# Residual rows of two matrix products added by accumulating DMA transfers instead of by VectorE

## The chip, the cores and the metric

The kernel runs on one core of one Trainium2 chip. A core has a matrix engine (TensorE, "PE" in the profile), three engines for elementwise work (VectorE "DVE", ScalarE "ACT", GpSimd "POOL"), and SyncE ("SP"), which in this kernel issues DMA transfers. Matmuls read SBUF and accumulate in PSUM banks. The engines run side by side and wait for each other through semaphores, and each works through its own queue in order. The metric is the time of one execution on the device in microseconds; lower is better.

## The reference

One decoder layer on 512 tokens of width 2048, in float32. What matters here:

```
h   = rms_norm(x, norm1_g)
mix = concat(gla_mixer(...), dilated_mixer(...))      # from h @ w_in
x   = x + mix @ w_out                                 # output product + residual
h2  = rms_norm(x, norm2_g)
x   = x + (silu(h2 @ w_gate) * (h2 @ w_up)) @ w_down  # last product + residual
```

w_out is 2048 x 2048, w_gate and w_up are 2048 x 5632, w_down is 5632 x 2048. Both additions of x are residuals: the product's result and the rows of x so far are added elementwise.

## The kernel before, in words

**Products by Strassen's scheme.** Every large product is cut into blocks of 512 output columns by 256 tokens and computed by the seven-product scheme of Strassen and Winograd. A `Pair` is one such unit: two blocks of 512 columns for two halves of 256 tokens, from the products P1, P5, P6, P3, P7, P2, P4 in this order (`PRODUCTS`). Each product runs over `op.groups` groups of rows (4, and 3 in the last two pairs of the last product). One product and one group is an item.

**An item.** The weights are loaded in quarters of 512 KB (`load_quarter`, line 222; tiles `wa` to `wd`), some are subtracted from each other on VectorE (line 256), ScalarE rounds the result to the matrix engine's format (`wh`, line 331), VectorE computes the rest (`wl`, line 335), and TensorE does 12 matmuls (line 361): 8 with `wh`, 4 with `wl`. `wh` and `wl` have two buffers each. The left operand is split into tiles `AA` and `AS` the same way (lines 174 and 175).

**Seeds and closes.** P1, P5 and P6 are first products: when one ends, `seeds` has ScalarE copy its two PSUM banks into SBUF tiles `seed` (line 280, or line 282 with a scale), m = 0 one item and m = 1 two items later. P2, P7 and P3 end a block: `close` adds the bank to the seed on VectorE (line 294, or 298 with a scale), and then `final(half, which, tiles, None)` gets the finished tiles. P1's seed is closed after P2, P5's after P7, and P6's after P3, the product that follows it. P4 ends the fourth block without a seed; there `final` gets the bank itself.

**Residuals.** In the output product (`final_out`, two pairs) and the last product (`final_down`, six pairs: three slices of the inner dimension by two column halves), `final` adds residual rows: rows of x in the first; rows of the stored x (`x1_d`) or of the sums so far (`y_d`) in the second. `begin` calls `ahead` three items after the start of P3, P7, P2 and P4, which loads two tiles of 128 x 512 from DRAM into the single buffers `q` and `k` (`residual_loads`, line 1313). `residual` then adds them on VectorE: to the closed seed (line 1325) for three blocks of a pair, and the bank to the loaded tile (line 1322) for P4's. The results are stored (lines 1354, 1541 and 1539).

**What the output product does besides.** Its `final` also squares the tiles for the next norm (ScalarE, line 1356), scales them with `prox` (line 1333; `prox` is computed on GpSimd, lines 158 and 159, from the first pair's sums), turns them on TensorE (line 1120) and sends them to DRAM tensors `xn_d`, from where they come back as operand parts of the gate and up products (`r`, `top`, `T`, `v`, lines 1184 and 1228). The first gate and up pair needs all of them. In the last product, operand parts come from `p_d` and `S_d` the same way while the pair before still runs.

**What sets the order.** After the first pair a scheduler places each engine's instructions, in the order of the calls as far as inputs and buffers allow by its own estimate. Each engine, and SyncE's queue of DMA issues, then runs in that order; an issue that waits for a buffer holds those behind it.

Of the kernel before, what the change touches and what calls it, by code (L numbers as in the profile page):

```python
# [14 lines left out]
ALU = mybir.AluOpType  # L15
# [3 lines left out]
P = 128  # L19
# [16 lines left out]
CLOSES = {"P3": (0, 1), "P7": (1, 1), "P2": (0, 0), "P4": (1, 0)}  # L36
# [71 lines left out]
def block_kernel(ctx: ExitStack, tc: tile.TileContext, ins, out):  # L108
    nc = tc.nc
    x, w_in, w_out, w_gate, w_up, w_down = (  # L110
        ins[n] for n in ("x", "w_in", "w_out", "w_gate", "w_up", "w_down")
    )
# [15 lines left out]
    def nm(s):  # L128
        uid[0] += 1
        return f"{s}_{uid[0]}"  # L130
# [7 lines left out]
    def work(tag, shape=(P, 512), bufs=1):  # L138
        return mp.tile(list(shape), F32, name=nm(tag), tag=tag, bufs=bufs)
# [6 lines left out]
    load = nc.sync.dma_start  # L146
# [10 lines left out]
    def rsqrt_mean(dst, src, n):  # L157
        nc.gpsimd.tensor_scalar(dst, src, 1.0 / n, EPS, op0=ALU.mult, op1=ALU.add)
        nc.gpsimd.tensor_tensor(dst, dst, mhalf[:, : dst.shape[-1]], op=ALU.pow)
# [69 lines left out]
    def unfolded(t):  # L229

        return t.rearrange("p (a b) -> p b a", b=2)

    def halves(t):
        return t.rearrange("p (b a) -> p b a", b=2)

    class Pair:
# [25 lines left out]
        def begin(self, prod):  # L262
            if prod == "P1":
                X = self.accs()
                self.dst = {"P1": X, "P6": X, "P7": X, "P4": X}
            elif prod == "P5":
                self.dst["P5"] = self.dst["P3"] = self.accs()
            elif prod == "P2":
                self.dst["P2"] = self.accs()
            ahead = getattr(self.final, "ahead", None)  # L270
            if ahead and prod in CLOSES:
                later(3, lambda: ahead(*CLOSES[prod]))

        def seeds(self, src, half):
            res = []

            def one(m):
                t = cpool.tile([P, 512], F32, name=nm("seed"), tag="C")
                if self.scale is None:
                    nc.scalar.copy(halves(t), unfolded(src[m]))  # L280
                else:
                    nc.scalar.activation(  # L282
                        halves(t), unfolded(src[m]), AF.Copy, scale=self.scale(half, m)
                    )
                res.append(t)

            later(1, lambda: one(0))
            later(2, lambda: one(1))
            return res
# [18 lines left out]
        def end(self, prod):  # L308
            src = self.dst[prod]
            if prod in ("P1", "P5", "P6"):  # L310
                self.held[prod] = self.seeds(src, int(prod == "P5"))
            elif prod == "P4":
                later(1, lambda: self.final(1, 0, None, src), hold=True)
            else:
                which = {"P3": "P6", "P7": "P5", "P2": "P1"}[prod]
                self.close(self.held[which], src, *CLOSES[prod])
# [181 lines left out]
    def later(units, fn, hold=False):  # L498

        deferred.append([units, fn, hold])  # L500
# [182 lines left out]
    for g in range(4):  # L683
        for b in (2 * g, 2 * g + 1):
            if g < 3:
                t = apool.tile([P, 2, 512], F32, name=nm("xT"), tag="A")
# [487 lines left out]

        soon(rest, 2)

    final_gate.ahead = onorm_load

    def part(src, half):
        def get(t=None):  # L1180
# [8 lines left out]
    def early_jobs(op, groups, tops, flip):  # L1189

        h0, h1 = (1, 0) if flip else (0, 1)
        jobs = [op.early(g, part(tops[g], h0), part(tops[g], h1)) for g in groups]
        next(jobs[0])
        yield
        for i, job in enumerate(jobs):
            if i + 1 < len(jobs):
                next(jobs[i + 1])
            next(job)
            yield 0.5
            next(job)  # L1200
            yield 0.5
# [103 lines left out]
    prox = const([P, 4], "prox")  # L1305
    rs2 = const([P, 4], "rs2")

    def residual_loads(rows, c0, src):

        res = []  # L1310
        for m in range(2):
            r = work(("q", "k")[m])
            load(r, src(rows[m], c0))
            res.append(r)
        return res

    def residual(tiles, acc_, rest):
        res = []
        for m in range(2):
            r = rest[m]  # L1320
            if tiles is None:
                nc.vector.tensor_tensor(halves(r), unfolded(acc_[m]), halves(r), op=ALU.add)
                res.append(r)
            else:
                nc.vector.tensor_tensor(tiles[m], tiles[m], r, op=ALU.add)  # L1325
                res.append(tiles[m])
        return res

    def scaled_store(tiles, rows, half, dsts, k0, tags=None):
        xs = []  # L1330
        for m in range(2):
            s = work(tags[m]) if tags else work("L", bufs=2)
            nc.scalar.activation(s, tiles[m], AF.Copy, scale=prox[:, rows[m] : rows[m] + 1])
            xs.append(s)
        return lambda: transposed_store(xs, half, dsts, g2[:, k0 : k0 + 4])

    def final_out(second):
        rest_of = {}

        def ahead(half, which):  # L1340
            tok = 1 - half
            rest_of[half, which] = residual_loads(
                [2 * tok, 2 * tok + 1], 512 * (2 * second + which),
                lambda t, c: x[t * P : (t + 1) * P, c : c + 512],
            )

        def final(half, which, tiles, acc_):
            tok = 1 - half
            rows = [2 * tok, 2 * tok + 1]
            ch = 2 * second + which  # L1350
            tiles = residual(tiles, acc_, rest_of.pop((half, which)))
            for m in range(2):
                t = rows[m]
                store(x1_d[t][:, 512 * ch : 512 * ch + 512], tiles[m])
                jk = work("st", (P, DV), bufs=2).bitcast(mybir.dt.bfloat16)
                nc.scalar.activation(
                    jk, tiles[m], AF.Square, accum_out=ss2[:, t, ch : ch + 1]
                )
            if second:
                turn = scaled_store(tiles, rows, tok, xn_d[2 * ch : 2 * ch + 2], 4 * ch)  # L1360

                def rest():
                    turn()
                    if which == 1 and half == 1:
                        background.append(early_jobs(opn, (2, 3), tops, False))
                        background.append(late_jobs(opn, ((2, 3),), tops, bots, False))

                later(2, rest)
                if which == 0 and half == 1:
                    output_scales()  # L1370
            elif which == 0 and half == 1:
                nc.vector.tensor_tensor(part2, ss2[:, :, 0], ss2[:, :, 1], op=ALU.add)
                rsqrt_mean(prox, part2, D // 2)
                background.append(first_columns())
                background.append(operand_jobs(opn, tops, bots, 0, 2))

        final.ahead = ahead
        return final

    def first_columns():  # L1380
        places = [(ch, tok) for ch in range(2) for tok in range(2)]
# [30 lines left out]
    def output_scales():  # L1412
        tmp2 = const([P, 4], "tmp2")
        nc.vector.tensor_tensor(tmp2, ss2[:, :, 2], ss2[:, :, 3], op=ALU.add)
        nc.vector.tensor_tensor(tmp2, tmp2, part2, op=ALU.add)
        rsqrt_mean(rs2, tmp2, D)
        nc.gpsimd.tensor_scalar(part2, part2, 2.0 / D, EPS, op0=ALU.mult, op1=ALU.add)
        nc.gpsimd.tensor_tensor(part2, part2, phalf, op=ALU.pow)
        nc.gpsimd.tensor_tensor(rs2, rs2, part2, op=ALU.mult)
# [92 lines left out]
    for j in range(11):  # L1512
        c = slice(512 * j, 512 * j + 512)
# [6 lines left out]
    y_d = [dram([P, D], f"y_d{t}") for t in range(4)]  # L1520

    def final_down(i, np_):
        rest_of = {}
        prev = x1_d if i == 0 else y_d

        def ahead(half, which):
            rest_of[half, which] = residual_loads(
                [2 * half, 2 * half + 1], 512 * (2 * np_ + which),
                lambda t, c: prev[t][:, c : c + 512],
            )  # L1530

        def final(half, which, tiles, acc_):
            rows = [2 * half, 2 * half + 1]
            c0 = 512 * (2 * np_ + which)
            tiles = residual(tiles, acc_, rest_of.pop((half, which)))
            for m in range(2):
                t = rows[m]
                if i == 2:
                    store(out[t * P : (t + 1) * P, c0 : c0 + 512], tiles[m])
                else:  # L1540
                    store(y_d[t][:, c0 : c0 + 512], tiles[m])

        final.ahead = ahead
        return final

    for i in range(3):
        g0 = 4 * i
        rows_d = [(512 * (g0 + g), 512 * (g0 + g) + 256) for g in range(opd[i].groups)]
        for np_ in range(2):
            c = 1024 * np_  # L1550
# [51 lines left out]
```

## Time and profile before

| | |
|---|---|
| median of 3 runs | 1977.21 us |
| lowest, highest | 1974.11, 1977.57 us |
| profiled execution | 1975.93 us, of it the span 1974.1 us |
| granted TensorE clock in it | 0.996 |
| TensorE, VectorE, ScalarE, GpSimd busy | 1932.0, 1655.0, 1094.1, 58.7 us |
| DMA moved | 360.45 MB, 57.3% of the DMA engines' time on SyncE's queue |

Times of rows are microseconds from the span's start. Of the two stages that the change touches, the output product lies at about 570 to 720, and the last product at about 1570 to 1970. A group's row gives the line, the engine, the operation, the tile written and those read, the shape, the count, then busy time and mean nanoseconds of one, then the idle time of the engine ahead of these instructions and what ended it. A row of the waits view gives who waited for whom: total, times, longest. A row of the timeline gives start, duration, engine, line, and in a bracket the idle time just before.

### The profile page before, as it was taken

Reading aid. Unit: us, or ns where it says so; the run is one execution under the profiler, and the core shown is the slowest. Engines: PE = TensorE matmul, PEld = TensorE weight load, DVE = VectorE, ACT = ScalarE, POOL = GpSimd, SP = SyncE. Lnnn points to the kernel's source line nnn. Section 1 sums busy time; section 2 is a strip of 40 time slices with the busy share of each in tenths; the row PEclk is TensorE's granted clock in tenths of the full one; section 3 lists DMA queues with packets and bytes.
Section 4 is the critical chain, followed back from the end, with each engine's and each line's share of the span. In section 5 each row is a group of like instructions: output and inputs, shape, how many; then the busy total and the mean of one; then the engine's idle time right before and its main releaser. Section 6 shows DMA issues by size and latency. Waiting matters only on the chain.

```text
span 1974.1 us, 25791 instructions
## 1 busy us (share of the span) xinstructions
PE 1932.0 (98%) x9226; PEld 1671.6 (85%) x9226; DVE 1655.0 (84%) x1850; ACT 1094.1 (55%) x1600; POOL 58.7 (3%) x81
## 2 busy tenths in 40 slices
PE   7999999999999999999999999999999999999998
PEld 6888888888878877888888888888888888888887
DVE  7997887868789789878878878878879989989987
ACT  6664564566766666545545545445446646546443
POOL 0000230010000000000000000000000000000000
PEclk9999999999999999999999999999999999999999
DMA  8358365374666685554554554554555855855762
GB/s 277 113 170 276 106 186 157 127 213 133 214 205 203 215 278 163 179 166 129 182 166 132 176 165 129 175 163 132 172 163 168 294 204 180 301 179 178 248 213 75
DMA packets 237113, 360.45 MB, mean 183 GB/s; under 512 B 18246, under 2 KB 96783, under 8 KB 236984
## 3 DMA queue, kind: packets, MB, share of 16 engines
q1 hardware_dynamic: 236776, 358.72, 57.3%
q8 instruction: 72, 1.18, 0.3%
q14 instruction: 57, 0.47, 0.1%
q10 hardware_dynamic: 208, 0.08, 0.0%
HBM read 296.59 MB, written 64.51 MB: 183 GB/s over the span
## 4 chain that ended last, share of the span: by engine, by line
PE 79%; DVE 8%; DMA 7%; issue 3%; ACT 2%; SPq 1%; POOL 1%; DVEq 0%; ACTq 0%
PE acc L361 71%; DVE wl L335 3%; PE acc L429 3%; DVE wa L256 1%; PE bank L1120 1%; PE bank L978 1%; ACT wh L331 1%; DMA wc<-in_w_in 1%; DVE AS L175 1%; DMA T<-p_d 1%; DMA x<-in_x 1%; DMA q<-y_d 0%; PE bank L1010 0%; DMA xn_d<-oT 0%; DVE seed L1325 0%
## 5 line engine op out<-in xcount | busy, mean ns | idle before, releaser
L361 PE MATMUL acc<-wh,AS 128*128 128x512 f32 x3008 | 712.0, 379 | 0.0
L361 PEld LDWEIGHTS acc<-wh,AS 128*128 128x128 f32 x3008 | 569.1, 189 | 81.7 <-ACT wh L331 0.6
L331 ACT CAST wh<-wa 128x1024 fp32r<-128x1024 f32 x376 | 393.6, 1048 | 384.2 <-PE acc L361 359.5
L361 PE MATMUL acc<-wh,AA 128*128 128x512 f32 x2256 | 536.4, 381 | 5.6 <-ACT wh L331 5.4
L335 DVE TENSOR_TENSOR wl<-wa,wh 128x1024 fp32r<-128x1024 f32 x376 | 457.4, 1220 | 72.0 <-ACT wh L331 46.5
L361 PEld LDWEIGHTS acc<-wh,AA 128*128 128x128 f32 x2256 | 426.7, 190 | 70.0 <-ACT wh L331 9.1
L361 PE MATMUL acc<-wl,AS 128*128 128x512 f32 x1504 | 395.7, 386 | 7.9 <-DVE wl L335 7.2
L361 PEld LDWEIGHTS acc<-wl,AS 128*128 128x128 f32 x1504 | 278.9, 189 | 61.7 <-DVE wl L335 20.9
L361 PE MATMUL acc<-wl,AA 128*128 128x512 f32 x1128 | 299.0, 388 | 6.1 <-DVE wl L335 6.1
L361 PEld LDWEIGHTS acc<-wl,AA 128*128 128x128 f32 x1128 | 210.7, 190 | 38.7 <-DVE wl L335 9.0
L331 ACT CAST wh<-wb 128x1024 fp32r<-128x1024 f32 x94 | 98.6, 1049 | 127.4 <-PE acc L361 122.7
L331 ACT CAST wh<-wc 128x1024 fp32r<-128x1024 f32 x94 | 98.4, 1047 | 106.8 <-PE acc L361 102.2
L331 ACT CAST wh<-wd 128x1024 fp32r<-128x1024 f32 x94 | 98.4, 1048 | 105.8 <-PE acc L361 102.3
L256 DVE TENSOR_TENSOR wa<-wc,wa 128x1024 f32<-128x1024 f32 x94 | 114.6, 1223 | 43.8 <-DMA wc<-in_w_gate 24.2
L335 DVE TENSOR_TENSOR wl<-wc,wh 128x1024 fp32r<-128x1024 f32 x94 | 114.8, 1221 | 38.6 <-ACT wh L331 38.6
L335 DVE TENSOR_TENSOR wl<-wd,wh 128x1024 fp32r<-128x1024 f32 x94 | 114.5, 1220 | 35.0 <-ACT wh L331 28.1
L335 DVE TENSOR_TENSOR wl<-wb,wh 128x1024 fp32r<-128x1024 f32 x94 | 113.9, 1219 | 6.1 <-ACT wh L331 6.1
L256 DVE TENSOR_TENSOR wb<-wd,wb 128x1024 f32<-128x1024 f32 x94 | 114.6, 1219 | 1.0 <-DMA wd<-in_w_in 0.5
L256 DVE TENSOR_TENSOR wa<-wb,wa 128x1024 f32<-128x1024 f32 x94 | 113.7, 1220 | 0.8
L256 DVE TENSOR_TENSOR wa<-wd,wa 128x1024 f32<-128x1024 f32 x94 | 113.1, 1218 | 0.1
L298 DVE SCALAR_TENSOR_TENSOR seed<-acc,rs,seed 128x512 f32<-128x512 f32 x96 | 70.5, 746 | 24.9 <-PE acc L361 24.9
L282 ACT ACTIVATE seed<-acc,rs 128x512 f32<-128x512 f32 x96 | 60.6, 681 | 1.4 <-PE acc L361 0.8
(289 smaller groups left out, 1367.4 us busy)
## 6 DMA issues: line engine op xcount, KB each, us to landing
wa<-in_w_gate SPq DMA_DIRECT2D x44, 512.0 KB, 4.4
wb<-in_w_up SPq DMA_DIRECT2D x44, 512.0 KB, 4.4
wd<-in_w_up SPq DMA_DIRECT2D x44, 512.0 KB, 4.5
wc<-in_w_gate SPq DMA_DIRECT2D x44, 512.0 KB, 3.6
wc<-in_w_in SPq DMA_DIRECT2D x28, 512.0 KB, 4.1
wa<-in_w_in SPq DMA_DIRECT2D x24, 512.0 KB, 5.2
wb<-in_w_in SPq DMA_DIRECT2D x24, 512.0 KB, 6.1
wd<-in_w_in SPq DMA_DIRECT2D x24, 512.0 KB, 6.0
```

What stands on the lines that cost most here:

```text
L175: nc.vector.tensor_tensor(a[:, :, 1, :], src, a[:, :, 0, :].bitcast(F32), op=ALU.subtract)
L256: nc.vector.tensor_tensor(src, self.quarter(one, g), src, op=ALU.subtract)
L282: nc.scalar.activation(halves(t), unfolded(src[m]), AF.Copy, scale=self.scale(half, m))
L298: nc.vector.scalar_tensor_tensor(halves(seed[m]), unfolded(src[m]), self.scale(half, m), halves(seed[m]), op0=ALU.mult, op1=ALU.add,)
L331: nc.scalar.copy(high[k], sources[k])
L335: nc.vector.tensor_tensor(low[k], sources.pop(k), high[k].bitcast(F32), op=ALU.subtract)
L361: nc.tensor.matmul(p.dst[prod][m], a[:, jj, hl, m * P : (m + 1) * P], folded(w[:, jj, :]), start=fresh and g == 0 and len(terms) == 2 and ...
L429: recent["pe"] = nc.tensor.matmul(dst[prod][m], a[:, jj, hl, m * P : (m + 1) * P], folded(w[:, jj, :]), start=fresh and g == 0 and len(ter ...
L978: nc.tensor.matmul(lp[:, :n], qh[:, b * P : (b + 1) * P], kh[:, :n], start=True, stop=True)
L1120: nc.tensor.transpose(bk[:, jj, m * P : (m + 1) * P], tiles[m][:, f : f + P], ident)
```

## The change

For three of the four blocks of a pair the residual rows are no longer loaded into `q` and `k` and added by VectorE. Instead, right after ScalarE's copy of the first product into its seed, GpSimd issues a DMA transfer that reads the residual rows from DRAM and adds them into the seed in SBUF (`accum_op=ALU.add`). The close adds the second bank to it as before, and its result holds the residual already. P4's block keeps its load and its add (lines 1320 and 1328 of the changed kernel). Pairs whose `final` has no `addend` keep their course. Per pair of the two products: 6 loads on SyncE's queue and 6 adds on VectorE fewer, 6 accumulating transfers on GpSimd's queue more; 48 each in all.

```diff
@@ Pair.begin
             ahead = getattr(self.final, "ahead", None)
-            if ahead and prod in CLOSES:
+            if ahead and prod in CLOSES and (CLOSES[prod] == (1, 0) or not self.final.addend):
                 later(3, lambda: ahead(*CLOSES[prod]))
@@ Pair.seeds
-        def seeds(self, src, half):
+        def seeds(self, src, half, which):
             res = []
+            addend = getattr(self.final, "addend", None)
             def one(m):
                 t = cpool.tile([P, 512], F32, name=nm("seed"), tag="C")
...
+                if addend:
+                    nc.gpsimd.dma_start(t, addend(half, which, m), accum_op=ALU.add)
                 res.append(t)
@@ Pair.end
-                self.held[prod] = self.seeds(src, int(prod == "P5"))
+                self.held[prod] = self.seeds(src, *{"P1": (0, 0), "P5": (1, 1), "P6": (0, 1)}[prod])
@@ residual_loads and residual become with_residual
+    def with_residual(final, src):
+        rest = []
+        def ahead(half, which):
+            for m in range(2):
+                r = work(("q", "k")[m])
+                load(r, src(half, which, m))
+                rest.append(r)
+        def whole(half, which, tiles, acc_):
             if tiles is None:
-                nc.vector.tensor_tensor(halves(r), unfolded(acc_[m]), halves(r), op=ALU.add)
-                res.append(r)
-            else:
-                nc.vector.tensor_tensor(tiles[m], tiles[m], r, op=ALU.add)
-                res.append(tiles[m])
+                tiles = rest
+                for m in range(2):
+                    r = tiles[m]
+                    nc.vector.tensor_tensor(halves(r), unfolded(acc_[m]), halves(r), op=ALU.add)
+            final(half, which, tiles)
+        whole.ahead, whole.addend = ahead, src
+        return whole
@@ final_out and final_down
-            tiles = residual(tiles, acc_, rest_of.pop((half, which)))
...
-        final.ahead = ahead
-        return final
+        return with_residual(final, rows_of_x)
...
+        return with_residual(final, sums_so_far)
```

More of the change, by code (lines that the diff above doesn't have):

```diff
@@ L1175, in final_gate @@
         soon(rest, 2)
-    final_gate.ahead = onorm_load
+    final_gate.ahead, final_gate.addend = onorm_load, None
     def part(src, half):
@@ L1306, in block_kernel @@
     rs2 = const([P, 4], "rs2")
[L1308 to L1313, printed above, removed]
-            res.append(r)
[L1315 to L1320, printed above, removed]
-            if tiles is None:
-                nc.vector.tensor_tensor(halves(r), unfolded(acc_[m]), halves(r), op=ALU.add)
-                res.append(r)
-            else:
-                nc.vector.tensor_tensor(tiles[m], tiles[m], r, op=ALU.add)
-                res.append(tiles[m])
-        return res
+    def with_residual(final, src):
[6 more added lines that the diff above has]
+        def whole(half, which, tiles, acc_):
+            if tiles is None:
+                tiles = rest
[5 more added lines that the diff above has]
+        return whole
     def scaled_store(tiles, rows, half, dsts, k0, tags=None):
@@ L1337, in final_out, with rows_of_x, final @@
     def final_out(second):
[L1338 to L1347, printed above, removed]
+        def rows_of_x(half, which, m):
+            t, c = 2 * (1 - half) + m, 512 * (2 * second + which)
+            return x[t * P : (t + 1) * P, c : c + 512]
+        def final(half, which, tiles):
             tok = 1 - half
@@ L1522, in final_down, with sums_so_far, final @@
     def final_down(i, np_):
-        rest_of = {}
         prev = x1_d if i == 0 else y_d
[L1526 to L1532, printed above, removed]
+        def sums_so_far(half, which, m):
+            c = 512 * (2 * np_ + which)
+            return prev[2 * half + m][:, c : c + 512]
+        def final(half, which, tiles):
             rows = [2 * half, 2 * half + 1]
             c0 = 512 * (2 * np_ + which)
-            tiles = residual(tiles, acc_, rest_of.pop((half, which)))
             for m in range(2):
@@ L1541, in final @@
                     store(y_d[t][:, c0 : c0 + 512], tiles[m])
-        final.ahead = ahead
-        return final
+        return with_residual(final, sums_so_far)
     for i in range(3):
```

## The prediction

> **What bounds the kernel now.** I read the busy shares first, then the same shares by stretch, then what TensorE waited for in the two stages that the change touches, then single instructions there. The page, its span, shares and chain:
>
> ```profile
> span 1974.1 us, 25791 instructions
> ...
> PE 1932.0 (98%) x9226; PEld 1671.6 (85%) x9226; DVE 1655.0 (84%) x1850; ACT 1094.1 (55%) x1600; POOL 58.7 (3%) x81
> ...
> PE 79%; DVE 8%; DMA 7%; issue 3%; ACT 2%; SPq 1%; POOL 1%; DVEq 0%; ACTq 0%
> ```
>
> TensorE is busy 98% of the span, and the change takes no matmul away. So all it can win is the time in which TensorE stands still near the residual adds, plus the tail. Busy time by stretch (start:end, length, then PE, PEld, DVE, ACT, POOL, clock, DMA share, GB/s); the output product's second half and the last product's pairs:
>
> ```profile
> 640.00:680.00 40.00, 37.66 (x189) 32.55 (x189) 34.06 (x33) 28.30 (x49) 2.96 (x2) 1.00 0.70 236
> 680.00:720.00 40.00, 38.08 (x175) 31.47 (x174) 34.91 (x43) 24.98 (x40) 0.00 (x0) 1.00 0.71 232
> 720.00:772.00 52.00, 46.23 (x208) 37.29 (x207) 44.87 (x55) 37.95 (x65) 4.41 (x5) 0.97 0.69 223
> 1632.00:1705.00 73.00, 71.07 (x328) 61.36 (x328) 70.30 (x79) 42.96 (x57) 0.00 (x0) 1.00 0.66 211
> 1780.00:1852.00 72.00, 70.80 (x327) 61.04 (x326) 70.03 (x78) 42.04 (x54) 0.00 (x0) 1.00 0.68 218
> 1964.00:1974.10 10.10, 4.77 (x23) 3.83 (x21) 2.91 (x4) 0.00 (x0) 0.00 (x0) 1.00 0.50 157
> ```
>
> In the last product VectorE is the fuller engine in two stretches (70.3 of 73 us), and TensorE still loses only 1.9 and 1.2 us there. What it waited for, by stretch (the waits view of TensorE for 640 to 680, for 680 to 720, and for 720 to 775; then three single gaps, the idle time in the bracket, and from the chain that ended last the load ahead of the third):
>
> ```profile
> PE bank L1120 <- ACT L L1333: 2.3, 2, 1.2
> ...
> PE acc L361 <- DVE wl L335: 1.7, 3, 0.8
> ...
> PE acc L361 <- DVE wl L335: 3.9, 2, 2.6
> PE acc L361 <- ACT wh L331: 1.1, 2, 0.9
> PE bank L1120 <- ACT L L1333: 0.5, 2, 0.3
> ...
> 752.03 2.00 PE L361 MATMUL acc<-wl,AA 128*128 128x512 f32 x4 [2.60 <-DVE wl L335]
> ...
> 1695.71 1.99 PE L361 MATMUL acc<-wh,AA 128*128 128x512 f32 x8 [1.93 <-ACT wh L331]
> ...
> 1836.12 5.43 DMA T<-p_d
> ...
> 1843.25 1.99 PE L361 MATMUL acc<-wh,AA 128*128 128x512 f32 x8 [1.20 <-ACT wh L331]
> ```
>
> **The change part by part.** *Removed.* 48 adds on VectorE (line 1325) and the 48 loads of their residual rows (line 1313, three of every four). By group of lines (count, busy us, mean ns, idle before), and the residual loads on SyncE with their time to landing:
>
> ```profile
> L1325 DVE TENSOR_TENSOR seed<-seed,k 128x512 f32<-128x512 f32 x24 | 16.5, 686 | 0.0
> L1325 DVE TENSOR_TENSOR seed<-seed,q 128x512 f32<-128x512 f32 x24 | 16.4, 684 | 1.0 <-DMA q<-in_x 0.9
> ...
> L1313 SPq DMA_DIRECT2D k<-x_d x8: 319/647/1874, 1566.0 to 1707.1; - x8
> ...
> DMA to landing us min/median/max: 2.9/5.4/7.5
> ```
>
> VectorE loses 16.5 + 16.4 = 32.9 us, or 6 x 0.685 = 4.1 us in each of eight pairs; SyncE loses 48 issues of about half a microsecond. In the built programs TensorE's order is unchanged row for row, ScalarE's counts are unchanged, and the 16 loads that stay (for P4) stand earlier in SyncE's queue, since no other load holds their two buffers.
>
> Where that meets a TensorE wait (rows of single instructions, idle in the bracket):
>
> ```profile
> 650.92 0.69 DVE L1322 TENSOR_TENSOR q<-acc,q 128x512 f32<-128x512 f32 x1 [1.94 <-DMA q<-in_x]
> ...
> 1686.06 0.50 SPq L1313 DMA_DIRECT2D q<-x_d  x1
> 1686.61 1.03 SPq L1313 DMA_DIRECT2D k<-x_d  x1
> 1687.75 0.67 SPq L1228 DMA_DIRECT2D T<-S_d  x1
> ...
> 1694.10 0.62 ACT L174 CAST AS<-T 128x512 fp32r<-128x512 f32 x1 [5.40 <-DMA T<-S_d]
> ```
>
> (a) 640 to 680: the add at 650.92 idled 1.94 us for its load; its result goes through `prox` on GpSimd to the scaled tiles that TensorE waits 2.3 us for. With the load early I take 2.0; bounds 0 and 2.3.
> (b) 680 to 720: the 1.7 us lie mostly ahead of the second pair's first close. I take 0; bounds 0 and 1.7.
> (c) 720 to 775: 3.9 + 1.1 + 0.5 = 5.5 us. VectorE gets 4.1 us back just ahead of them, but the operand parts also go out to DRAM and back here, which the change leaves. I take half, 2.7; bounds 0 and 5.5.
> (d) Last product: the T load at 1687.75 stands behind two residual loads (0.50 + 1.03 us) and behind VectorE work that two adds (1.37 us) had pushed back; ScalarE idles 5.40 us for it and TensorE 1.93. These 2.9 us go, so the 1.93 us gap goes; the 1.20 us at 1843.25 follows a late T load too (landed 1841.55), one block on. I take 3.0 of 1.93 + 1.20 = 3.13; bounds 0 and 3.1. What is late next is the cast itself, whose input is the matmul's own release, so no stall behind it.
> (e) The tail:
>
> ```profile
> 1967.74 1.03 PE L361 MATMUL acc<-wl,AA 128*128 128x512 f32 x4
> ...
> 1969.20 0.69 DVE L1322 TENSOR_TENSOR q<-acc,q 128x512 f32<-128x512 f32 x1 [3.61 <-DMA q<-y_d]
> ```
>
> The last matmuls end at 1968.77, the add starts at 1969.20 because its load lands then. With the load long done it starts at about the matmul's end: 0.4; bounds 0 and 0.6. The two adds and the store behind it stay.
>
> Gain: 2.0 + 0 + 2.7 + 3.0 + 0.4 = 8.1 us; at most 2.3 + 1.7 + 5.5 + 3.1 + 0.6 = 13.2.
>
> *Added.* 48 transfers of 256 KB that add into the seed, issued by GpSimd behind ScalarE's copy; the close on VectorE now waits for each. Behind the waiting close stands the next `wl` on VectorE, and TensorE waits for that. P1's and P5's seeds have two or more products of time; P6's is closed one product later. The copies and first closes of P6's seed in three pairs (output product's second, last product's first, last product's fifth), then a `wl` right behind a close and the load that uses it one item on:
>
> ```profile
> 689.10 1.06 ACT L280 COPY seed<-acc 128x512 f32<-128x512 f32 x2
> 701.93 0.69 DVE L294 TENSOR_TENSOR seed<-acc,seed 128x512 f32<-128x512 f32 x1
> ...
> 1595.21 1.07 ACT L280 COPY seed<-acc 128x512 f32<-128x512 f32 x2
> 1608.53 1.28 DVE L294 TENSOR_TENSOR seed<-acc,seed 128x512 f32<-128x512 f32 x2
> ...
> 1882.49 1.07 ACT L280 COPY seed<-acc 128x512 f32<-128x512 f32 x2
> 1889.96 0.69 DVE L294 TENSOR_TENSOR seed<-acc,seed 128x512 f32<-128x512 f32 x1 [0.93 <-PE acc L361]
> ...
> 1953.66 1.22 DVE L335 TENSOR_TENSOR wl<-wc,wh 128x1024 fp32r<-128x1024 f32 x1
> ...
> 1957.17 0.84 PEld L361 LDWEIGHTS acc<-wl,AA 128*128 128x128 f32 x4
> ```
>
> From the end of the first copy (0.53 us after the start) to the close: 12.3 us, 12.8 us and 6.9 us (three groups there instead of four). In the last two pairs a late close has 1957.17 - 1954.88 = 2.3 us more before TensorE feels it, so 9.2 us in all.
>
> No accumulating transfer and no transfer issued by GpSimd is in this trace. Its nearest rows are the plain loads of the same size (2.9 to 7.5 us) GpSimd's own small instructions, and the stores of the seeds (line 1541), for the second leg that an add needs:
>
> ```profile
> L159 POOL TENSOR_TENSOR ss<-ss,mhalf x16: 1006/1007/1922, 244.4 to 461.9; 128x4 f32<-128x4 f32 x16
> L159 POOL TENSOR_TENSOR prox<-prox,mhalf x1: 1865/1865/1865, 657.0 to 657.0; 128x4 f32<-128x4 f32 x1
> ...
> DMA to landing us min/median/max: 2.2/4.4/7.6
> ```
>
> Low end: 1.0 + 2.9 = 3.9 us. High end: 1.9 + 7.5 + a median store's 4.4 = 13.8 us. My value is 1.5 + 5.4 = 6.9 us, a median load with GpSimd's step in front, since each transfer moves what the removed load moved. At 6.9 us no close is late: cost 0. At 13.8 us it would be 2 x (13.8 - 9.2) = 9.2, plus 2 x 1.5 = 3.0 in the output product, plus 4 x 1.0 = 4.0 in the last product's first four pairs: 16.2 us. GpSimd works in order: `prox` and the scales of the next stage stand behind six accumulates each, which wait only for copies tens of microseconds older; hidden, and if not, it lengthens wait (a) directly.
>
> One rule weighed here, which nothing above needs: the Trainium skill, "DMA: Bandwidth & Descriptors", section "Anatomy of one DMA", fits a GpSimd-issued transfer as 2.0 us plus its bytes at 436 GB/s, which gives an estimate of 2.6 us for 256 KB, a cost of 0 as well; no run here shows it yet, and the loads' 5.4 us beside weight traffic say that the fit is too low here.
>
> Sum: 1975.93 (this execution, 1974.1 of it span) - 8.1 = 1967.8 us. The median of the runs shown, 1977.21, lies 1.28 above that execution; against the median it is 1977.21 - 8.1 = 1969.1 us, my prediction.
>
> **The rivals.**
>
> *The waits refill (no change).* In 640 to 772 TensorE waits for parts that travel to DRAM and back, and removing VectorE work ahead of them moves only when VectorE idles. For it: VectorE is only 85 to 87% busy there (34.06 of 40, 34.91 of 40). Against it: the 1.94 us idle at 650.92 is for a residual load. Then (a) to (c) give nothing and (d) and (e) stay: 1977.2 - 3.4 = 1973.8 us. A difference within 0.2%, 4.0 us, is about what a measurement of this kernel can't tell from none.
>
> *Late accumulates (slower).* The mechanism is one: a P6 seed's accumulate lands after its close is due, VectorE stands, `wl` is late. For it: one form of GpSimd instruction took 1.01 to 1.92 us for no cause that its row shows, and VectorE, beside which GpSimd would have to prepare the transfers, is 96 and 97% busy in two stretches. It decides when cost exceeds gain by 4.0: with 2 (t - 9.2) + 2 (t - 12.3) + 4 (t - 12.8) = 12.1, t is 13.3 us. At the high end of 13.8 the time is 1969.1 + 16.2 = 1985.3 us; each further microsecond adds 8.
> The page that bears on this is the Trainium skill, "SBUF — State Buffer", section "A bandwidth-pool intuition that's wrong (but worth ruling out)": a GpSimd transfer of about 620 ns took about 3100 ns beside VectorE copies that hold the shared port, since descriptors couldn't be written. Its section "Who interferes with whom" says that tensor_tensor has no such mode and takes only the read side; VectorE's rows here are TENSOR_TENSOR, so by that rule this rival is the less likely.
>
> *All of it counts.* Every wait of (a) to (e) goes: 1977.2 - 13.2 = 1964.0 us. Against it: (b) lies ahead of the closes.
>
> **How the numbers follow.** The forecast, 1964 to 1973, holds 0.58 with the full-gain case inside it; no change 0.18; late accumulates 0.24, of which half lie under 1986. The range 1964 to 1986 leaves out some 0.12 above and 0.05 below. Likeliest case's own range: 1964 to 1973. Faster 0.58, same 0.18, slower 0.24.
>
> **What would show it.** Right: GpSimd issues 48 transfers with landing under 9 us; the closes idle for TensorE, not for a DMA; the gaps at about 1695 and 1843 are gone; the P4 add near 650 no longer idles; 2 to 5 us less idle TensorE in 640 to 772. Wrong: VectorE idle before the closes with the accumulate as releaser, first in the last two pairs, with TensorE waiting for `wl` behind them; or the 2.60 us gap near 752 as large as before.

## The result and the profile after

The changed kernel takes 1986.42 us (median of 5 runs, 1984.26 to 1987.24); the kernel before took 1975.56 us beside it (5 runs, 1974.11 to 1977.57). The ratio is 1.0055, 95% interval 1.0042 to 1.0067: 10.9 us slower. The forecast was 1969.1 us.

The page of the kernel after: span, TensorE's busy time, the two DMA queues that matter (packets, MB, share of 16 engines; `q1` is SyncE's queue, `q0` GpSimd's), and the shares of the chain:

```profile
span 1985.5 us, 25843 instructions
...
PE 1935.1 (97%) x9226; PEld 1673.4 (84%) x9226; DVE 1627.1 (82%) x1802; ACT 1096.1 (55%) x1600; POOL 101.0 (5%) x129
...
q1 hardware_dynamic: 229864, 346.13, 54.8%
q0 software_dynamic: 6912, 12.59, 3.9%
...
PE 81%; DMA 8%; DVE 6%; issue 2%; ACT 2%; SPq 1%; POOL 0%; DVEq 0%; ACTq 0%; POOLq 0%
```

VectorE is 27.9 us less busy, as it was meant to be, TensorE has the same 9226 matmuls in the same order, and the span is 11.4 us longer. The new queue moves the same 12.59 MB that SyncE's queue lost.

Do the closes wait for the adds? The closes (line 299 of the changed kernel) with what ended their idle time (us, times), then the transfers (line 289) with the GpSimd time that one takes to issue and the time to landing:

```profile
L299 DVE TENSOR_TENSOR seed<-acc,seed x48: 678/684/692, 622.9 to 1974.7; 128x512 f32<-128x512 f32 x48
...
  PE acc L366: 11.5, 14
  DMA seed<-y_d: 0.3, 1
```

```profile
L289 POOL DMA_DIRECT2D seed<-y_d x24: 862/886/1165, 1734.4 to 1951.6; - x24
...
DMA to landing us min/median/max: 3.6/6.3/8.6
```

No: once, for 0.3 us, in 48 closes. A transfer lands 6.3 us after its issue, close to the 6.9 us that the prediction took for issue and landing. The new time is elsewhere. Busy time by stretch, for the output product's second half (columns as in the prediction), and TensorE's waits in these three stretches:

```profile
640.00:680.00 40.00, 36.47 (x176) 31.43 (x175) 30.76 (x30) 25.85 (x43) 4.79 (x4) 0.97 0.66 204
680.00:720.00 40.00, 32.56 (x134) 26.44 (x133) 25.33 (x30) 21.38 (x35) 3.51 (x4) 0.90 0.71 198
720.00:790.00 70.00, 67.02 (x317) 56.16 (x317) 63.57 (x75) 51.10 (x83) 4.67 (x5) 1.00 0.61 203
```

```profile
PE acc L366 <- ACT wh L336: 2.8, 1, 2.8
PE bank L1125 <- ACT L L1338: 0.8, 1, 0.8
...
PE acc L366 <- DVE wl L340: 6.2, 3, 4.2
PE acc L366 <- ACT wh L336: 1.1, 1, 1.1
...
PE acc L366 <- DVE wl L340: 2.5, 4, 1.2
PE bank L1125 <- ACT L L1338: 0.2, 1, 0.2
```

From 680 to 720 TensorE waits 7.3 us where it waited 1.7 before, and runs 134 matmuls in place of 175. The chain that ended last (start, length, what) goes through transfers here. Its three longest from 665 to 707 in the kernel after, then the same store and the same `wc` load in the kernel before:

```profile
669.56 6.76 DMA v<-x_d
...
683.29 7.52 DMA xn_d<-oT
...
698.89 7.63 DMA wc<-in_w_out
```

```profile
679.39 4.35 DMA xn_d<-oT
...
691.82 4.26 DMA wc<-in_w_out
```

All three are on SyncE's queue, and GpSimd issues an adding transfer beside each: P1's second at 668.93, P5's two from 681.29, P6's two from 697.16. The median landing of `v` from 640 to 720 is 2.9 us before. In the last product there are small new gaps ahead of `wl`, two or three in each of the first four pairs; one each of the first, the second and the fourth:

```profile
1614.50 1.13 PE L366 MATMUL acc<-wl,AS 128*128 128x512 f32 x4 [0.95 <-DVE wl L340]
...
1692.35 1.13 PE L366 MATMUL acc<-wl,AS 128*128 128x512 f32 x4 [1.34 <-DVE wl L340]
...
1841.60 1.13 PE L366 MATMUL acc<-wl,AS 128*128 128x512 f32 x4 [1.45 <-DVE wl L340]
```

What made `wl` late is in the same chain around the first of these gaps:

```profile
1604.31 1.24 DVE wl L340
...
1605.56 6.50 DMA wc<-in_w_down
...
1613.23 1.23 DVE wl L340
...
1614.47 3.76 DMA wc<-in_w_down
```

`wc` is a quarter of the weights on SyncE's queue. Its issue waits for a buffer that the `wl` before sets free, so it is loaded just in time: here 6.50 us pass to its landing, and VectorE needs it for the next `wa` and `wl`. At the same place before, TensorE ran without a gap. The median landing of these loads in the last product's first five pairs (1590 to 1900), first of the kernel before, then of after:

```profile
wc<-in_w_down SPq DMA_DIRECT2D x19, 512.0 KB, 4.2
```

```profile
wc<-in_w_down SPq DMA_DIRECT2D x19, 512.0 KB, 6.5
```

Since TensorE's order is the same in all kernels of this study, the same matmul can be looked up in each trace. This table gives how much later (or earlier, with a minus) than in the kernel before it starts, at the output product's start and end (571 and 775 us of before) and the last product's start and end (1566 and 1968), in us, and what each stage adds. Each row is one execution, and runs of one kernel spread over some 5 us. The two kernels whose output product is as before (last product, P1 and P5; own tiles, last product) differ from before there by 1.6 and 0.3 us, so that a difference of a microsecond or two says nothing.

| kernel | 571 | 775 | 1566 | 1968 | output product | last product |
|---|---|---|---|---|---|---|
| after | -0.2 | 7.8 | 7.6 | 12.1 | +8.0 | +4.5 |
| without transfers | 0.0 | -5.2 | -6.1 | -10.0 | -5.2 | -3.9 |
| transfers copy | 0.4 | 3.3 | 2.4 | 0.3 | +2.9 | -2.1 |
| without P6 | 0.2 | 4.1 | 3.5 | -0.2 | +3.9 | -3.7 |
| P6 only | -1.0 | 2.7 | 2.4 | 5.5 | +3.7 | +3.1 |
| last product, P1 and P5 | -0.5 | 1.1 | 0.3 | -3.0 | +1.6 | -3.3 |
| loads, no adds | 2.5 | 4.1 | 3.2 | 1.8 | +1.6 | -1.4 |
| adds, no loads | -1.3 | -4.3 | -4.4 | -7.9 | -3.0 | -3.5 |
| own tiles, both products | 0.4 | 4.3 | 4.5 | 1.0 | +3.9 | -3.5 |
| own tiles, last product | -0.8 | -1.1 | -1.2 | -4.7 | -0.3 | -3.5 |

### The profile page after: what moved, and what is told of

It reads as the page before. It is cut to its first block, busy times and chain, and to the rows that moved or that the text cites. A ratio compares the mean times of both kernels' runs of the same rounds, so it can differ in the third digit from the quotient of the medians.

```text
span 1985.5 us, 25843 instructions
## 1 busy us (share of the span) xinstructions
PE 1935.1 (97%) x9226; PEld 1673.4 (84%) x9226; DVE 1627.1 (82%) x1802; ACT 1096.1 (55%) x1600; POOL 101.0 (5%) x129
## 3 DMA queue, kind: packets, MB, share of 16 engines
q0 software_dynamic: 6912, 12.59, 3.9%
## 4 chain that ended last, share of the span: by engine, by line
PE 81%; DMA 8%; DVE 6%; issue 2%; ACT 2%; SPq 1%; POOL 0%; DVEq 0%; ACTq 0%; POOLq 0%
PE acc L366 73%; DVE wl L340 3%; PE acc L434 3%; DMA wc<-in_w_down 1%; PE bank L1125 1%; DVE wa L256 1%; DVE AS L175 1%; PE bank L983 1%; DMA wc<-in_w_in 1%; PE bank L1015 1%; DMA x<-in_x 1%; DMA xn_d<-oT 1%; DMA mix_d<-r 1%; DMA v<-x_d 1%; ACT wh L336 1%
```

## The experiments

The theory formed from the two traces (theory A in the expectations; A1 is its narrower form, that P6's transfers do it): the transfers on GpSimd's queue share the DMA engines with SyncE's loads, and the loads that are just in time, `wc` above all and the operand parts that come back from DRAM, land later; the removed work was worth about what was predicted. What its rivals would give stands in the expectations. Each ratio is to runs of the kernel before on the same chip, whose medians were 1974.91 us (the first four kernels below), 1974.65 (the next four), 1974.15 (the two that split the removed work) and 1974.27 (the last one, and the repeat).

**Without the transfers.** Everything of the change but the 48 transfers.

```diff
-                if addend:
-                    nc.gpsimd.dma_start(t, addend(half, which, m), accum_op=ALU.add)
```

> The changed kernel without its 48 accumulating transfers; the residual rows of three of four blocks are left out of the result. Every other engine's order stays row for row. Theory A (the transfers share the DMA engines with loads that TensorE's chain needs just in time): the loads land as early as before and the time falls to 1965 to 1970 us, 16 to 21 us under the changed kernel's 1986.4 and below the 1975.6 of before. Theory B (the new order of the queues costs, the transfers don't): 1984 to 1988 us.

Measured: 1967.2 us, ratio 0.9965 (0.9953 to 0.9978), 7.7 us faster than before. The instructions of the other engines come in after's order, so the whole loss, 0.9% of the time, lies in the transfers. SyncE's queue, and TensorE's waits in the last product (1550 to 1970):

```profile
q1 hardware_dynamic: 229864, 346.13, 54.1%
...
PE acc L364 <- DVE wl L338: 0.9, 3, 0.4
```

The 3.4 us that TensorE waits there for `wh` before are gone, and of gaps like the new ones of after there are three left, of 0.4 us at most.

**The transfers copy in place of adding.** Same transfers, same queue, same places.

```diff
-                    nc.gpsimd.dma_start(t, addend(half, which, m), accum_op=ALU.add)
+                    nc.gpsimd.dma_start(t, addend(half, which, m))
```

> The changed kernel with the same 48 transfers on the same queue, but as plain copies: they overwrite the seed, so the first product of three of four blocks is left out of the result. Order row for row as in the changed kernel. Theory A with the add as the cost (an added byte takes 1.95 times the engine time of a loaded one, by the queues' shares): half the excess goes, about 1976 to 1980 us. Theory A with the place and the queue as the cost (any 256 KB put beside a just-in-time load): 1983 to 1987 us. Theory B: 1984 to 1988 us.

Measured: 1974.86 us, ratio 0.9999 (0.9989 to 1.0008), a little under the range given for the add as the cost: more than half of the excess went. Its GpSimd queue, then one issue and the landing (line 289):

```profile
q0 software_dynamic: 3840, 12.59, 1.9%
```

```profile
L289 POOL DMA_DIRECT2D seed<-y_d x24: 536/538/548, 1726.0 to 1939.8; - x24
...
DMA to landing us min/median/max: 2.9/3.6/6.9
```

So the 12.59 MB cost 7.7 us on this queue as plain copies, all that was won, and making them add costs some 11 us more (1.0055 - 0.9999 is 0.56% of 1975 us). The add is dear on the DMA engines: 6912 packets in place of 3840, 3.9% of the engines' time in place of 1.9%, 0.89 us of GpSimd per issue in place of 0.54, and 6.3 us to landing in place of 3.6. Worked out: 3.9% of 16 x 1985.5 us over 48 transfers is 25.8 us of engine time for one, or 1.6 us if all 16 work on it; a copy by the same sum 0.8 us.

**One product alone.** A set names the blocks whose seed gets its rows by a transfer; the others load and add as before. First the output product alone, then the last product alone.

```diff
-                if addend:
+                if addend and (half, which) in self.final.adding:
...
-        return with_residual(final, sums_so_far)
+        return with_residual(final, sums_so_far, set())   # and the other way round
```

> The change in the output product alone; the last product loads and adds as before. By the shift of the matmuls in the changed kernel against before (7.8 us at the first matmul after the operand parts of the gate and up products) both theories give 1975.6 + 7.8 = 1983 us, give or take 2. If the parts don't add up, 1976 to 1980.

> The change in the last product alone. By the shift of the matmuls (7.6 us at the start of the last product, 12.2 at its end, and 1 us less in the tail) 1975.6 + 4.6 - 1 = 1979 us, give or take 2. Loads of wc land 6 us or more after their issue beside P6's accumulates if theory A holds, 3.5 to 4 us if B does.

Measured: 1984.08 us, ratio 1.0044 (1.0030 to 1.0057), and 1977.58 us, ratio 1.0008 (0.9998 to 1.0019). The two losses, 0.44 and 0.08%, add up to after's 0.55% within their intervals. Most of it is made by the 12 transfers of the output product's two pairs; in the last product 36 transfers cost about what the stage gained.

**By block.** P1's and P5's seeds by transfer and P6's block as before (32 transfers), and the reverse (16).

```diff
-        return with_residual(final, rows_of_x, {(0, 0), (1, 1), (0, 1)})
+        return with_residual(final, rows_of_x, {(0, 0), (1, 1)})   # P6 only: {(0, 1)}; sums_so_far the same
```

> P1's and P5's seeds get their residual by accumulating transfers in both products, P6's block loads and adds as before: 32 transfers instead of 48. Theory A1 (P6's transfers do the harm, since they run while the wc quarters of the product after it are loaded just in time): 1971 to 1976 us. Theory A2 (each transfer does about the same harm): two thirds of the excess over the kernel without transfers, 1967.2 + 13 = 1980 us, plus the 16 adds and loads that come back, 1982.

> The counterpart: accumulating transfers for P6's seeds alone, 16 instead of 48; the other blocks as before. Theory A1: most of the excess stays, 1982 to 1986 us. Theory A2: 1975 + a third of the 11 us, about 1978 us.

Measured: 1974.77 us, ratio 0.9999 (0.9989 to 1.0008), and 1982.45 us, ratio 1.0039 (1.0025 to 1.0052). The third of the transfers that belongs to P6 does most of the harm. In the last product the split is plain in the table: -3.7 us without P6's, +3.1 with P6's alone. In the output product it isn't: +3.9 and +3.7, so P1's and P5's cost there too.

**Last product, P1 and P5 alone.** 24 transfers.

```diff
-        return with_residual(final, rows_of_x, {(0, 0), (1, 1)})
+        return with_residual(final, rows_of_x, set())
```

> Accumulating transfers only in the last product and only for P1's and P5's seeds (24). In the changed kernel the last product's matmuls fall behind beside P6's transfers (1.2, 1.0, 1.6 and 1.7 us) and once beside P1's of the first pair (1.2). Theory A1: the two gaps of ScalarE go and only the 1.2 us stays, 1972 to 1974 us. Theory A2: 1976 to 1978 us.

Measured: 1970.25 us, ratio 0.9982 (0.9972 to 0.9993), less than either theory gave. A second time:

> The faster variant once more, beside the one above on the same chip: adding transfers for P1's and P5's seeds in the last product alone. Expected as in its first run, 1969 to 1972 us, ratio about 0.998; if its gain was chance, ratio 1.000.

Measured: 1970.39 us, ratio 0.9983 (0.9974 to 0.9993). This beats both kernels, the one before by 0.17%, the changed one by about 0.7% (0.9983 against 1.0055). Why P6's transfers hurt and these don't is in the order of SyncE's weight loads. The weight loads of after around the first pair's transfers (rows of line 222 on SyncE), and GpSimd's transfers for P1, P5 and P6:

```profile
1567.38 0.37 SPq L222 DMA_DIRECT2D wd<-in_w_down  x1
1603.42 11.42 SPq L222 DMA_DIRECT2D wc<-in_w_down  x4
```

```profile
1583.11 1.82 POOL L289 DMA_DIRECT2D seed<-x_d  x2 [821.86 <-ACT seed L283]
1594.54 1.75 POOL L289 DMA_DIRECT2D seed<-x_d  x2 [9.62 <-ACT seed L283]
1605.17 1.74 POOL L289 DMA_DIRECT2D seed<-x_d  x2 [8.88 <-ACT seed L283]
```

Between 1567.38 and 1603.42 no weight quarter is loaded: P1's and P5's transfers, at 1583 and 1594, meet none, and in the trace it is so in all six pairs. P6's, at 1605.17, meet the four `wc` loads that start at 1603.42; they meet `wc` loads in the first four pairs, `wa` loads in the fifth and no weight load in the sixth. Two of them, by the sum above, hold the engines for 2 x 1.6 = 3.2 us; the `wc` load issued between them took 6.50 us, and before the loads at that place took 3.5 to 3.7. The chain over the same place, with P6's transfers alone and then with P1's and P5's alone:

```profile
1596.38 3.64 DMA wc<-in_w_down
...
1602.44 5.37 DMA wc<-in_w_down
```

```profile
1589.93 25.25 PE acc L366 x117
```

And the landings of `wc` from 1590 to 1900, in the same order:

```profile
wc<-in_w_down SPq DMA_DIRECT2D x19, 512.0 KB, 5.9
```

```profile
wc<-in_w_down SPq DMA_DIRECT2D x19, 512.0 KB, 4.0
```

With P1's and P5's alone TensorE runs through; with P6's alone the chain goes through two `wc` loads. By the Trainium skill, "DMA: Bandwidth & Descriptors", section "Issuing engines are not separate DMA queues", transfers issued by different engines run on the same 16 DMA engines and interleave; the landings agree (4.2 before, 6.5 with all transfers, 5.9 with P6's, 4.0 without them). With all 48 as copies the same median is 4.3 us. One new gap doesn't belong to this: that of 1.08 us in after near 1592 stands beside P1's transfers, but the kernel without the adds, which has no transfer on GpSimd's queue, has one of 2.66 us at the same matmul.

**Own tiles instead of transfers.** No transfer; the kernel before, but P4's residual rows go to the seeds' pool in the output product, and in the last product each block has two tiles of its own.

```diff
-            r = work(("q", "k")[m])
+            if tags == "C":
+                r = cpool.tile([P, 512], F32, name=nm("res"), tag="C")
+            else:
+                r = work(tags[m], bufs=2 if tags[m] == "L" else 1)
...
+                "C" if (half, which) == (1, 0) else ("q", "k"),        # final_out
...
+                {(0, 1): ("q", "k"), (1, 1): ("oT", "PT"), (0, 0): ("L", "L"), (1, 0): "C"}[half, which],  # final_down
```

> No GpSimd transfers and every add as before; only the residual rows' tiles change: P4's go into the seeds' pool, and in the last product each block has its own pair of tiles, so that a load never waits for the add of the block before. It tests whether the part of the gain that came from late residual loads can be had without accumulating transfers. If the late loads were that part: 1970 to 1973 us. If what counts is VectorE's adds and the number of loads on SyncE's queue, no change, 1974 to 1976 us.

Measured: 1972.61 us, ratio 0.9993 (0.9983 to 1.0002): not told apart from no change, though in the table the last product gains 3.5 us and the output product loses 3.9. The traced execution was the slowest of its ten, 3.7 us above the median, and in it GpSimd's first `prox` instruction took 4.50 us where it took 1.10 before, so that the 3.9 can't be taken for the kernel's own.

**Which part of the removed work was worth something.** The kernel before without the 48 adds, and the kernel before with the adds but without their loads.

```diff
-                nc.vector.tensor_tensor(tiles[m], tiles[m], r, op=ALU.add)
```

```diff
-            if ahead and prod in CLOSES:
+            if ahead and prod in CLOSES and (CLOSES[prod] == (1, 0) or not getattr(self.final, "lean", 0)):
...
-                nc.vector.tensor_tensor(tiles[m], tiles[m], r, op=ALU.add)
+                nc.vector.tensor_tensor(tiles[m], tiles[m], tiles[m], op=ALU.add)
```

> The kernel before without the 48 adds of line 1325; all residual loads stay on SyncE's queue, and the residual of three of four blocks is left out of the result. It asks where the 7.7 us come from that the changed kernel gained when its transfers were left out: VectorE's 32.9 us, or the 12.6 MB that no longer move. Theory V (VectorE's time, as the prediction reasoned for the gaps of 680 to 775 and near 1695 and 1843): most of the gain is here too, 1966 to 1970 us, ratio about 0.9965. Theory L (the bytes): 1973 to 1976 us, ratio about 1.000. If each does half, about 1971 us.

> The counterpart: the 48 adds stay on VectorE, but add the closed seed to itself, and their 48 residual loads are left out (P4's stay), so the residual of three of four blocks is left out of the result. Theory V: no gain but what the late T loads give in the last product, 1972 to 1976 us, ratio 0.9985 to 1.000. Theory L: most of the gain, 1966 to 1970 us, ratio about 0.9965. If each does half, about 1971 us.

Measured: 1973.16 us, ratio 0.9992 (0.9981 to 1.0003), and 1968.77 us, ratio 0.9972 (0.9961 to 0.9983). The busy times of the first:

```profile
PE 1929.1 (98%) x9226; PEld 1672.2 (85%) x9226; DVE 1627.0 (82%) x1802; ACT 1095.7 (55%) x1600; POOL 64.8 (3%) x81
```

VectorE is as free as in after (1627.0 against 1627.1 us), and no gain can be told from none; without the loads, and with VectorE as full as before, there are 0.28 of the 0.35% that both together gave. Both times lie in the ranges of theory L: the gain of the kernel without transfers came mostly with the 48 loads that were gone, not with VectorE's time. But a load that is gone takes away its bytes and its place in SyncE's queue, where it waits for `q` or `k`, so this doesn't show yet that it was the bytes.

**The last product's gain without transfers.** The own tiles in the last product alone: the edit above without its line in the output product.

```diff
-                "C" if (half, which) == (1, 0) else ("q", "k"),        # final_out as before
```

> No transfer that adds. The kernel before with one edit in the last product: each block's residual rows get tiles of their own (q and k, oT and PT, two of L, two of the seeds' pool), so no residual load waits in SyncE's queue for the add of the block before; the output product is as before. It asks whether the gain that the changed kernel makes in the last product (the gaps near 1695 and 1843 gone, 3.1 to 3.5 us) needs the transfers at all. If it comes from the order in SyncE's queue: about 1971 us, ratio 0.998. If it needs VectorE's time: 1974 to 1975 us, ratio 1.000.

Measured: 1971.01 us, ratio 0.9983 (0.9974 to 0.9993), the same as the variant with P1's and P5's transfers beside it. So what can be won in the last product needs no transfer that adds, and no bytes fewer either: all 48 loads are still there, and what the edit takes away is their wait for `q` and `k`. That speaks against the bytes of theory L in this stage; for the output product no run parts the two.

## Why the prediction was wrong, by its own steps

**(a) 640 to 680, gain 2.0 of 2.3: the wait went, and another came.** P4's rows are there in time; the add starts without idle time (VectorE, line 1328):

```profile
651.02 0.68 DVE L1328 TENSOR_TENSOR q<-acc,q 128x512 f32<-128x512 f32 x1
```

TensorE's wait for the scaled tiles fell from 2.3 to 0.8 us, 1.5 where 2.0 was taken. But a wait of 2.8 us for `wh` came: ScalarE, which makes `wh`, stood 2.3 us for the `v` that took 6.76 us to land.

**(b) 680 to 720, gain 0, bounds 0 and 1.7: outside its bounds.** 1.7 us became 7.3, behind the store of 7.52 us and the `wc` load of 7.63 us shown above. The bounds held no loss, though the operand parts' way through DRAM was named under (c) as a limit.

**(c) 720 to 775, gain 2.7 of 5.5: the size came out by luck, the reason was wrong.** 2.7 us of waits are left in that stretch in after. The prediction gave the gain to the 4.1 us of VectorE's time. But in the kernel without transfers, where VectorE has the same time back, the gap of 2.60 us at 752.03 is as large as before:

```profile
746.96 1.18 PE L364 MATMUL acc<-wl,AA 128*128 128x512 f32 x4 [3.06 <-DVE wl L338]
```

It is small (0.59 us in after, 0.8 to 1.6 in the others) in the kernels with transfers in the output product, where TensorE comes to it late by the new waits. That VectorE uses this delay to get ahead fits, but isn't shown. The run with the adds gone and the loads kept won nothing in the output product (+1.6 in the table), the run with the loads gone and the adds kept did (-3.0), each in one execution.

**(d) Last product, gain 3.0: right.** The gaps at 1695.71 and 1843.25 of before are gone in after; at those matmuls its delay shrinks by 2.1 and 1.4 us. Two reasons were named, two residual loads ahead of the T load and two adds ahead of its use, and taking away either is enough (both gaps are 0.2 us or less with the adds gone and with the loads gone).

**(e) Tail, gain 0.4: right.** From the start of the last matmuls to the add are 0.85 us, 1.46 before, so 0.6 us was gained:

```profile
1979.88 1.03 PE L366 MATMUL acc<-wl,AA 128*128 128x512 f32 x4
1980.73 0.69 DVE L1328 TENSOR_TENSOR q<-acc,q 128x512 f32<-128x512 f32 x1 [3.52 <-PE acc L366]
```

**The sum of the gain, 8.1, and the 7.7 measured without transfers agree by luck.** In the trace without transfers TensorE's waits from 560 to 790 add up to 14.0 us where before has 15.5: 1.5 less, where (a) to (c) had 4.7. In the last product they fall from 3.6 to 0.9, close to (d). Most of the rest between these two traces is no wait at all: TensorE is busy 1926.8 us in place of 1932.0 with the same matmuls, and that sum differs between runs of one kernel too (1929.7 and 1926.7 us in the two of P1 and P5 in the last product).

**Added, cost 0: the step that failed.** It reads "a median load with GpSimd's step in front, since each transfer moves what the removed load moved. At 6.9 us no close is late: cost 0." The landing was right (6.3 us) and so was the slack (0.3 us of waits). Wrong was that a transfer's cost is the wait for that transfer. Its cost is what it does to the loads that share the DMA engines with it: 7.7 us as a copy and some 11 us more as an add. The prediction's high end, too, goes through late closes alone; no bound was set for what the transfers do to SyncE's loads, although the DMA share of 0.66 to 0.71 stands in the prediction's own rows. The second premise fell too: an adding transfer doesn't move what a load moves, but takes twice the engines' time of a copy of the same bytes.

**The rivals.** "Late accumulates" had the sign, the blocks (P6 above all) and nearly the time, 1985.3 against 1986.4 us, by a mechanism that did not occur: closes 0.3 us late in all, transfers that land in 8.6 us at most where 13.3 was needed. That its time is so near is luck. GpSimd's longer issue (0.86 to 1.2 us) is no sign of VectorE holding it up either, since as copies the same transfers take 0.54 us beside the same VectorE work. "The waits refill" was right that freeing VectorE alone wins nothing that can be told from none in the output product (+1.6 with the adds gone). It gave (a) nothing, where 1.5 us of the wait went, and had no loss in it.

## What to carry to other kernels

A transfer that takes no engine's time still takes the DMA engines': before moving work to one, list the loads that land just in time around each place where it will be issued, and price it by their delay, not only by its own deadline. Here 24 adding transfers placed where no weight quarter is loading, in the last product, came out ahead by 0.17%, and P6's 12, 10 of which meet weight loads, gave that back. The same gain was to be had by giving each block's residual rows tiles of their own, which is the cheaper trial: it asks first whether a load was late for its buffer or for the engine.

## What the runs showed of the hardware that was not expected

**A transfer that adds costs twice a copy on the DMA engines.** 144 packets against 80 per 256 KB (6912 and 3840 over 48), 25.8 against 12.5 us of engine time, 6.3 against 3.6 us to landing, 0.89 against 0.54 us of GpSimd to issue. Why it lands that late is not settled by these runs; the traffic beside it is the same in both.

**After some stalls TensorE runs at half pace for a while.** Rows of after, the gaps of 2.77 and 1.82 us, then the one of 4.23 us with what follows it:

```profile
678.06 3.39 PE L366 MATMUL acc<-wh,AS 128*128 128x512 f32 x8 [2.77 <-ACT wh L336]
...
695.86 1.13 PE L366 MATMUL acc<-wl,AS 128*128 128x512 f32 x4 [1.82 <-DVE wl L340]
...
708.96 2.08 PE L366 MATMUL acc<-wl,AS 128*128 128x512 f32 x4 [4.23 <-DVE wl L340]
710.83 3.62 PE L366 MATMUL acc<-wh,AS 128*128 128x512 f32 x8
714.25 1.43 PE L366 MATMUL acc<-wl,AS 128*128 128x512 f32 x4
```

Eight matmuls take 1.9 to 2.0 us elsewhere and four 1.0 to 1.1. Behind the gap of 4.23 us the first four come 468 ns apart ((710.83 - 708.96) / 4) and the next eight 428 ns ((714.25 - 710.83) / 8), where some 216 is usual, and the granted clock of the stretch is 0.90. The extra time is 1.4 us behind the first gap, none behind the second and 0.95 + 1.63 + 0.30 = 2.9 us behind the third, so the output product's loss of 8 us against before is some 5.5 us more waits (21.0 against 15.5 us from 560 to 790) and about 4.3 us of slow matmuls, some 1.8 us of it matched by the slow ones behind the gap of 2.60 us at 752.03 of before. The Trainium skill, "TensorE: Matmul & The Clock Gate", section "Part 1: The HAM clock gate (the "warmup" mystery)", says that the clock falls to half after a window of about 3.4 us without work and comes back after about as long of work; the gaps of 4.23 and 1.82 us agree, the one of 2.77 us was already enough, and behind the one of 4.23 us the slow pace lasted some 6 us, so here the measurement decides. The length of the gap alone doesn't settle it: one of 2.06 us (own tiles instead of transfers, at 740.02) has eight matmuls of 3.68 us behind it, one of 3.20 us (own tiles, last product, at 750.11) has eight of 1.89 us.

**What stays open.** In the output product P1's and P5's transfers cost as much as P6's (+3.9 and +3.7 us), through chains of several transfers (operand parts by way of DRAM, then `wc`). The trace of after shows one slow transfer beside each of the three, but how much of the stage's 8 us each of them makes was not measured apart. That a slower or later issue of P6's transfers would spare the `wc` loads wasn't tried.
